# Gate rows and head factors spread by DMA, and the relative-position product moved ahead of the input's transposes

## The chip, the cores and the metric

One core of one Trainium2 chip runs the whole program. The metric is the device time of one execution in microseconds; less is better.

## What is computed

The input x is 256 tokens of 1024 channels in fp32. The first block (block 1) is what the change touches:

```
u = rmsnorm(x) * norm_in;  p = u @ w_in          # 13 projections in one matrix
mLSTM: q, k (4 heads x 128, convolved over 4 tokens, SiLU), v (4 x 256), gates li, lf (4 each)
       num / max(|den|, exp(-m)) per head and token, normalised, times the output gates mo and mz
sparse attention, 8 heads x 64: index score I[t,s] = sum_h w[t,h] relu(iq[t,h] . ik[s]);
       each query attends to its top 64 admissible keys:
       softmax(q.k/8 + rel_bias[bucket(t - s)]) v, times the gate az
out = concat(mLSTM, attention) @ w_out + x, then a gated per-layer input
```

A second block of two layers follows (modulated norms, latent and block-sparse attention, convolved feed-forward), whose modulation vectors silu(c) @ mod_w are worked out in the background during block 1. Nothing of the second block is changed.

## The kernel before

**Tiles.** Activations stand transposed: 8 tiles of 128 channels x 256 tokens (u), each as a high part and the rounding rest. A weight tile is loaded in fp32 (raw, six buffers), cast by ScalarE to its high part (wh, line 174) and subtracted by VectorE to its rest (wl, line 175); four buffers each. A projection tile of 128 output channels is 8 channel blocks times the three products of lines 187 to 189 (high x high, high x rest, rest x high), 24 instructions of 256 columns; where tokens are on the partitions (av, mv) it is lines 213 to 215 with 512 columns. So TensorE needs one split from VectorE and one cast from ScalarE for every 12 products.

**Order.** Up to the ixq projection the order is written out by hand (`manual_schedule`, in block1). From there on a scheduler fixes one list per engine when the kernel is built; each engine goes through its list in order and waits at an instruction until what it reads, and the buffer it writes, is there. Program order and the generator `side()` (line 642), which `tick()` advances after each projection tile, give the scheduler its priorities. The projections run as: ixq (by hand), ikg (index keys and gates), aqk (8 tiles), av, mqk (8 tiles), mv, az (4), mo (8), mz (8).

**Beside the projections.** `side()` makes the gate rows (grow), the gates' running sums and maxima (gr, gB, ga, gM, gbm, lines 656 to 665), sends the maxima through DRAM to all partitions (mscr, mbc, lines 667 and 669, on GpSimd's queue), then the index scores of two query blocks (lines 679 to 688), the transposed gates (gcol), the top-k as eight rounds of MAX and MATCH_REPLACE per block (lines 704, 706) and the mask neg (713, 714). Once av is done it yields one attention stage per tick: logits lg (729), mask plus bias mb on GpSimd (733), the softmax' first step lgs on VectorE (334), exp on ScalarE (335), reciprocal and scaling pr on VectorE (337, 338), then one stage later the transposes ptr (740), pt, and another stage later hav (749, 750). After mv come the mLSTM stages: sums and numerators (mnum, lines 781 to 788), denominators through a transpose (mstT, 806; den, 810 to 814), mrT (820), rrow (822).

**Background.** Each mqk tile is convolved by one ScalarE and three VectorE steps (cv, line 863) and goes through a tanh. A modulation unit either makes 32 products on TensorE (line 983, ps_mod) or, with VectorE, eight accumulations of 1024 columns (modacc, one by ScalarE at line 996, seven by VectorE at line 998) and four products; either way VectorE reads the sum (modr, 1008), TensorE transposes it (modt, 1011) and VectorE copies it (mod, 1013). Its weight tiles (raw_mod) share the six raw buffers with the projections.

**What the change touches.** The gate rows are 8 of the 16 rows of g16 (line 633): two products with rows of the identity bring rows 8 to 11 and 12 to 15 to partitions 0 to 3 in PSUM (646, 647), and VectorE copies them to grow (653). The head factors rrow, 4 x 256, are spread over 128 partitions by four products with a broadcast identity column (826), and VectorE multiplies the eight halves of the numerators by them from PSUM (829). The bias of the relative position is a product of a 32 x 384 one-hot matrix (oh) with the bias table (rb), line 437, copied to relrow (439), sent to DRAM (relscr, 441) and read back as eight shifted 128 x 256 tiles (relb, two DMAs, 445). The names in the lists below carry the scheduler's tile numbers; the numbers of before and after differ by a few for the same tile.

Of the kernel before, what the change touches and what calls it, by code (L numbers as in the profile page):

```python
# [9 lines left out]
F32 = mybir.dt.float32  # L10
# [3 lines left out]
ALU = mybir.AluOpType  # L14
# [4 lines left out]
P = 128  # L19
S = 256  # L20
# [383 lines left out]
def vec(ap, s):  # L404
    return ap.rearrange(s, p=P)
# [3 lines left out]
def setup_first(g):  # L409
    nc, a = g.nc, g.a  # L410
    g.ident = g.mask("ident", 1.0, 0, 1, -1, cmp=ALU.not_equal)
    g.mhalf = g.cp.tile([P, 8], F32, tag="mhalf", name="mhalf")
    nc.gpsimd.memset(g.mhalf, -0.5)
    g.ones = g.cp.tile([P, P], F32, tag="ones", name="ones")
    nc.gpsimd.memset(g.ones, 1.0)


def setup_block1(g):
    nc, a, wk = g.nc, g.a, g.wk
    c = g.columns(g.rows([vec(a["m_norm"][0], "(k p) -> k p"), vec(a["norm_final"], "(k p) -> k p"),  # L420
                   vec(a["conv_w"][0], "j (k p) -> (j k) p")], "0"), "0", "A")
    g.m_norm, g.norm_final = c[:, 0:8], c[:, 8:16]
    g.conv_w = c[:, 16:48].rearrange("p (j k) -> p j k", j=4)
    g.anti = g.mask("anti", 1.0, -(P - 1), 1, 1, cmp=ALU.not_equal, pool=wk)
    g.rmask = g.mask("rmask", -BIG, P - 1, -1, -1, pool=wk)
    g.gbias = wk.tile([16, 1], F32, tag="gbias", name="gbias")
    nc.gpsimd.memset(g.gbias, 0.0)
    nc.sync.dma_start(g.gbias[8:16, :], a["b_gate"][0].rearrange("(k o) -> k o", o=1))
    g.zero4 = g.t1("zero4")[0:4]
    nc.gpsimd.memset(g.zero4, 0.0)  # L430

    oh = g.t3("oh")[0:32]
    rb = wk.tile([32, 8], F32, tag="rb", name="rb")
    nc.sync.dma_start(oh, a["buckets"])
    nc.sync.dma_start(rb, a["rel_bias"])
    ps = g.ps("relb", "A")
    nc.tensor.matmul(ps[0:8, 0:384], rb, oh, start=True, stop=True)
    row = g.t3("relrow")[0:8]
    nc.vector.tensor_copy(row, ps[0:8, 0:384])
    scr = g.dp.tile([8, 384], F32, tag="relscr", name="relscr")  # L440
    nc.gpsimd.dma_start(scr, row)
    g.relb = []
    for e in range(2):
        t = g.b4r(f"relb{e}").rearrange("p (h s) -> p h s", h=4)
        nc.gpsimd.dma_start(t, bass.AP(scr.tensor, scr.offset + 4 * e * 384, [[1, P], [384, 4], [1, S]]))
        g.relb += [t[:, h, :] for h in range(4)]
# [83 lines left out]
def block1(g):  # L530
    nc, a = g.nc, g.a
    V, A, T, G_ = nc.vector, nc.scalar, nc.tensor, nc.gpsimd
# [6 lines left out]
    with g.tc.manual_schedule():  # L539
        for tb in range(2):  # L540
            nc.sync.dma_start(xt[tb], a["x"][0, tb * P:(tb + 1) * P, :])
        norm_in = g.rows([vec(a["norm_in"][0], "(k p) -> k p")], "n", nc.scalar)
        setup_first(g)
        raws = [g.wload(w, 2 * c, 2, 6152, 512, f"ixq{c}") for c in range(4)]
        ws = []
# [33 lines left out]
        for _ in range(WARM):  # L579
            T.matmul(warm[:, 0:P], g.ident, g.ident, start=True, stop=True)  # L580
        g.norm_in = g.columns(norm_in, "n", "M")
        pst = [g.ps(f"xtr{i}", "A") for i in range(4)]

        def trans(k, tb):
# [8 lines left out]
        for k in range(KD):  # L593
# [11 lines left out]
            for e, f in ((0, 0), (0, 1), (1, 0)):  # L605
                for i in range(4):
# [3 lines left out]
                             stop=k == KD - 1 and (e, f) == (1, 0), skip_group_check=True)  # L610
# [8 lines left out]
    nc.sync.dma_start(rv[:, :, 72:80], w[:, 4096:4104].rearrange("(k p) c -> p k c", p=P))  # L619
    hv, lv = g.split(rv, "ikg")  # L620
    setup_block1(g)
    psk = g.ps("ikg", "M")
    for k in range(KD):
# [8 lines left out]
    g16, g16r = g.t1("g16")[0:16], g.t1("g16r")[0:16]  # L632
# [9 lines left out]
    def side():  # L642


        ps = g.ps("grow", "A")
        T.matmul(ps[0:4, 0:S], g.ident[0:16, 8:12], g16, start=True, stop=True)
        T.matmul(ps[0:4, S:2 * S], g.ident[0:16, 12:16], g16, start=True, stop=True)
        for tb in range(2):
            psw = g.ps(f"iwt{tb}", "A")
            T.transpose(psw[:, 0:16], g16r[:, tb * P:(tb + 1) * P], g.ident[0:16, 0:16])  # L650
            V.tensor_scalar(iw[:, tb, :], psw[:, 0:8], 8.0 ** -0.5, 0.125, op0=ALU.mult, op1=ALU.mult)
        grow = g.b2("grow")[0:4]
        V.tensor_copy(grow, ps[0:4, :])
        li, fr = grow[:, 0:S], grow[:, S:2 * S]
        r1, r2, Bc, ar, Mx, bm = (g.t1(n)[0:4] for n in ("gr1", "gr2", "gB", "ga", "gM", "gbm"))
        V.tensor_scalar(r2, fr, -1.0, None, op0=ALU.mult)
# [17 lines left out]
        for tb in range(2):  # L674
            n = (tb + 1) * P
            sc = g.t1(f"sc{tb}")
            for h in range(8):
                ps = g.ps(f"sc{tb}_{h}", "A")
# [12 lines left out]
        ps = g.ps("gcol", "A")  # L691
# [29 lines left out]
        for st in range(10):  # L721
            h = st
            if h < 8:
                lo = 64 * (h % 2)
                ps = g.ps(f"lg{h}", "A")
# [10 lines left out]
            h = st - 1  # L736
# [6 lines left out]
            h = st - 2  # L743
# [16 lines left out]
        for st in range(5):  # L760
            h = st
# [13 lines left out]
            h = st - 1  # L775
# [44 lines left out]
            T.transpose(prt[0:4, tb * P:(tb + 1) * P], rs[:, 4 * tb:4 * tb + 4], g.ident)  # L820
        rrow = g.t1("rrow")[0:4]
        V.tensor_scalar(rrow, prt[0:4, 0:S], 0.25, None, op0=ALU.mult)
        yield
        for h in range(4):
            pb = g.ps(f"mrb{h}", "A")
            T.matmul(pb[:, 0:S], g.ident[0:4, h:h + 1].to_broadcast([4, P]), rrow, start=True, stop=True)
            for vv in range(2):
                t = nums[h][:, vv * S:(vv + 1) * S]
                V.tensor_tensor(t, t, pb[:, 0:S], op=ALU.mult)
            if h % 2:  # L830
                yield

    iw = g.wk.tile([P, 2, 8], F32, tag="iw", name="iw")
    steps = side()
    n_tick = [0]

# [61 lines left out]
    ps = g.ps("ptT", "A")  # L898
# [621 lines left out]
```

## Time and profile before

| | |
|---|---|
| median of 3 runs | 877.22 us (877.14 to 877.37) |
| the profiled execution's own time | 879.18 us |
| its span, first to last instruction | 877.4 us |
| TensorE busy | 859.3 us, 98% |
| VectorE busy | 673.2 us, 77% |
| ScalarE busy | 502.6 us, 57% |
| GpSimd busy | 52.6 us, 6% |
| mean granted TensorE clock | 0.996 of full speed |

The profile covers one execution. Busy time tells how much of the span an engine worked; which engine sets the end of a stretch is read from who waits for whom there. TensorE's products are pipelined, so the price of one is taken from its start to the start of the next, not from its own duration, which reaches over the next one's start. A product of two fp32 operands is recorded twice.

### The profile page before, as it was taken

The page shows a single profiled execution, that of the slowest core. Times are in us where ns is not written, and L with a number is a line of the kernel's source. Part 1 is how long each engine was busy: PE and PEld are TensorE (multiplying, and loading weights), DVE is VectorE, ACT ScalarE, POOL GpSimd, SP SyncE. Part 2 cuts the span into 40 slices and gives each one's busy share as a digit, 9 for nine tenths or more (in the row PEclk, how much of TensorE's full clock was granted, in tenths as well). Part 3 has the DMA queues.
Part 4 walks back from the last instruction along what each step waited for, and adds up shares of the span by engine and source line. Part 5 has one row for each costly group of instructions (what it writes and reads, how often), then busy time and mean ns, then how long its engine had stood idle before and what let it go on. Part 6 is the DMA issues. An engine that isn't in the chain of part 4 may idle for free. (4 is left out here: it accounts for less than half of the span.)

```text
span 877.4 us, 14288 instructions
## 1 busy us (share of the span) xinstructions
PE 859.3 (98%) x5415; PEld 741.1 (84%) x5415; DVE 673.2 (77%) x1289; ACT 502.6 (57%) x925; POOL 52.6 (6%) x81
## 2 busy tenths in 40 slices
PE   9999999999999899999999999999999999999996
PEld 8998779999888688798888888678888988888885
DVE  5798787768767576679899998675866686777786
ACT  6555666445557555377556557276553775565660
POOL 2003111000000131000000000000000000000003
PEclk9999999999999999999999999999999999999999
DMA  8955796854447963498898985498453956566411
GB/s 269 357 197 175 279 345 202 285 211 151 144 150 258 305 250 117 132 377 286 305 331 296 336 290 190 162 345 296 161 176 104 377 178 203 181 220 204 143 49 48
DMA packets 112760, 199.27 MB, mean 227 GB/s; under 512 B 8388, under 2 KB 76468, under 8 KB 112692
## 3 DMA queue, kind: packets, MB, share of 16 engines
q1 hardware_dynamic: 111892, 196.25, 65.7%
q0 software_dynamic: 496, 1.59, 0.5%
q8 instruction: 42, 0.69, 0.3%
q10 hardware_dynamic: 304, 0.53, 0.2%
q14 instruction: 26, 0.21, 0.1%
HBM read 197.28 MB, written 1.08 MB: 226 GB/s over the span
## 5 line engine op out<-in xcount | busy, mean ns | idle before, releaser
L194 PE MATMUL ps_f<-ln,wh_f 128*128 128x512 f32 x576 | 203.8, 396 | 0.0
L195 PE MATMUL ps_f<-ln,wl_f 128*128 128x256 f32 x576 | 161.4, 280 | 0.0
L194 PEld LDWEIGHTS ps_f<-ln,wh_f 128*128 128x128 f32 x576 | 108.1, 188 | 26.5 <-issue 0.8
L195 PEld LDWEIGHTS ps_f<-ln,wl_f 128*128 128x128 f32 x576 | 108.7, 189 | 1.4 <-issue 0.4
L174 ACT CAST wh_fo<-raw_fo 128x1024 fp32r<-128x1024 f32 x38 | 39.9, 1050 | 39.3 <-PE ps_f L194 38.2
L174 ACT CAST wh_f<-raw_fa 128x1024 fp32r<-128x1024 f32 x36 | 37.7, 1051 | 40.8 <-PE ps_f L194 20.3
L175 DVE TENSOR_TENSOR wl_fo<-raw_fo,wh_fo 128x1024 fp32r<-128x1024 f32 x38 | 46.5, 1223 | 19.0 <-ACT wh_fo L174 18.9
L175 DVE TENSOR_TENSOR wl_f<-raw_fa,wh_f 128x1024 fp32r<-128x1024 f32 x36 | 43.9, 1222 | 15.3 <-ACT wh_f L174 15.3
L174 ACT CAST wh_f<-raw_fb 128x1024 fp32r<-128x1024 f32 x36 | 37.1, 1050 | 28.0 <-PE ps_fy L215 17.8
L998 DVE SCALAR_TENSOR_TENSOR modacc<-raw_mod,c,modacc 128x1024 f32<-128x1024 f32 x40 | 51.1, 1278 | 2.0 <-ACT modacc L996 2.0
L175 DVE TENSOR_TENSOR wl_f<-raw_fb,wh_f 128x1024 fp32r<-128x1024 f32 x36 | 43.4, 1221 | 9.2 <-ACT wh_f L174 8.9
L188 PE MATMUL ps_fi<-ln,wh_fi 128*128 128x256 f32 x128 | 35.6, 285 | 0.0
L215 PE MATMUL ps_fy<-wh_fo,fh 128*128 128x512 f32 (+1 forms) x99 | 35.2, 369 | 0.0
L214 PE MATMUL ps_fy<-wl_fo,fh 128*128 128x512 f32 (+1 forms) x99 | 35.1, 368 | 0.0
L189 PE MATMUL ps_fi<-ln,wl_fi 128*128 128x256 f32 x128 | 34.6, 283 | 0.0
L187 PE MATMUL ps_fi<-ln,wh_fi 128*128 128x256 f32 x128 | 34.0, 286 | 0.0
L213 PE MATMUL ps_fy<-wh_fo,fh 128*128 128x512 f32 (+1 forms) x99 | 33.3, 367 | 0.0
L204 DVE TENSOR_TENSOR adf<-ps_f,adf 128x256 f32<-128x256 f32 x72 | 30.0, 417 | 0.0
L983 PE MATMUL ps_mod<-raw_mod,c 128*32 128x256 f32 x400 | 26.9, 383 | 1.0 <-DVE mod L1013 1.0
L203 ACT COPY adf<-ps_f 128x256 f32<-128x256 f32 x72 | 26.1, 363 | 0.0
L174 ACT CAST wh_fi<-raw_fi 128x1024 fp32r<-128x1024 f32 x16 | 17.0, 1079 | 14.9 <-PE ps_mlay L215 8.3
L188 PEld LDWEIGHTS ps_fi<-ln,wh_fi 128*128 128x128 f32 x128 | 24.5, 192 | 0.4 <-DVE ln L377 0.4
(807 smaller groups left out, 2582.4 us busy)
## 6 DMA issues: line engine op xcount, KB each, us to landing
raw_mod<-in_mod_w_dram SPq DMA_DIRECT2D x48, 1024.0 KB
raw_fo<-in_ffn_w_out_dram SPq DMA_DIRECT2D x22, 1024.0 KB
raw_fa<-in_ffn_w_in_dram SPq DMA_DIRECT2D x18, 1024.0 KB
raw_fb<-in_ffn_w_in_dram SPq DMA_DIRECT2D x18, 1024.0 KB
raw_fi<-in_ffn_w_in_dram SPq DMA_DIRECT2D x16, 512.0 KB
raw_wo<-in_w_out_dram SPq DMA_DIRECT2D x6, 1024.0 KB
raw_aqk<-in_w_in_dram SPq DMA_DIRECT2D x4, 1024.0 KB
raw_mqk<-in_w_in_dram SPq DMA_DIRECT2D x4, 1024.0 KB
```

Source lines behind the costliest of these rows:

```text
L174: self.nc.scalar.copy(hv, src)
L175: self.nc.vector.tensor_tensor(lv, src, hv.bitcast(F32), op=ALU.subtract)
L187: T.matmul(ps, wh, xh, start=start, stop=False, skip_group_check=chk)
L188: T.matmul(ps, wh, xl, start=False, stop=False, skip_group_check=chk)
L189: T.matmul(ps, wl, xh, start=False, stop=stop, skip_group_check=chk)
L194: T.matmul(ps, wh, x[2], start=start, stop=False, skip_group_check=True)
L195: T.matmul(ps[:, 0:S], wl, x[0], start=False, stop=stop, skip_group_check=True)
L204: V.tensor_tensor(t, ps[:, 0:S], t, op=ALU.add)
L213: T.matmul(ps, xh, wh, start=start, stop=False)
L214: T.matmul(ps, xh, wl, start=False, stop=False)
L215: return T.matmul(ps, xl, wh, start=False, stop=stop)
L998: nc.vector.scalar_tensor_tensor(st["acc"], rv[:, e], c, st["acc"], op0=ALU.mult, op1=ALU.add)
```

## The change

The two loads of the relative position move from SyncE's queue to ScalarE's, and are issued early; the product, its copy and its three DMAs move from setup_block1 into the part whose order is written by hand, behind the column transposes of norm_in and ahead of the transposes of x. The two products for the gate rows and the copy give way to two DMAs from g16 to grow on GpSimd's queue. The four products for the head factors give way to a DMA of rrow to DRAM (rscr) and one that reads it back to all partitions (mrbc, 128 x 1024), both on GpSimd's queue; the eight multiplications read mrbc in SBUF. Lines below the edits have numbers higher by 8 to 10 in the changed kernel.

```diff
--- before.py
+++ after.py
@@ -429,11 +429,19 @@
     g.zero4 = g.t1("zero4")[0:4]
     nc.gpsimd.memset(g.zero4, 0.0)
 
-    oh = g.t3("oh")[0:32]
-    rb = wk.tile([32, 8], F32, tag="rb", name="rb")
-    nc.sync.dma_start(oh, a["buckets"])
-    nc.sync.dma_start(rb, a["rel_bias"])
-    ps = g.ps("relb", "A")
+
+def relative_load(g):
+
+    oh, rb = g.t3("oh")[0:32], g.wk.tile([32, 8], F32, tag="rb", name="rb")
+    g.nc.scalar.dma_start(oh, g.a["buckets"])
+    g.nc.scalar.dma_start(rb, g.a["rel_bias"])
+    return oh, rb
+
+
+def relative(g, oh, rb):
+
+    nc = g.nc
+    ps = g.ps("relb", "V")
     nc.tensor.matmul(ps[0:8, 0:384], rb, oh, start=True, stop=True)
     row = g.t3("relrow")[0:8]
     nc.vector.tensor_copy(row, ps[0:8, 0:384])
@@ -540,6 +548,7 @@
         for tb in range(2):
             nc.sync.dma_start(xt[tb], a["x"][0, tb * P:(tb + 1) * P, :])
         norm_in = g.rows([vec(a["norm_in"][0], "(k p) -> k p")], "n", nc.scalar)
+        buckets = relative_load(g)
         setup_first(g)
         raws = [g.wload(w, 2 * c, 2, 6152, 512, f"ixq{c}") for c in range(4)]
         ws = []
@@ -579,6 +588,7 @@
         for _ in range(WARM):
             T.matmul(warm[:, 0:P], g.ident, g.ident, start=True, stop=True)
         g.norm_in = g.columns(norm_in, "n", "M")
+        relative(g, *buckets)
         pst = [g.ps(f"xtr{i}", "A") for i in range(4)]
 
         def trans(k, tb):
@@ -642,15 +652,13 @@
     def side():
 
 
-        ps = g.ps("grow", "A")
-        T.matmul(ps[0:4, 0:S], g.ident[0:16, 8:12], g16, start=True, stop=True)
-        T.matmul(ps[0:4, S:2 * S], g.ident[0:16, 12:16], g16, start=True, stop=True)
+        grow = g.b2("grow")[0:4]
+        for e in range(2):
+            nc.gpsimd.dma_start(grow[:, e * S:(e + 1) * S], g16[8 + 4 * e:12 + 4 * e, :])
         for tb in range(2):
             psw = g.ps(f"iwt{tb}", "A")
             T.transpose(psw[:, 0:16], g16r[:, tb * P:(tb + 1) * P], g.ident[0:16, 0:16])
             V.tensor_scalar(iw[:, tb, :], psw[:, 0:8], 8.0 ** -0.5, 0.125, op0=ALU.mult, op1=ALU.mult)
-        grow = g.b2("grow")[0:4]
-        V.tensor_copy(grow, ps[0:4, :])
         li, fr = grow[:, 0:S], grow[:, S:2 * S]
         r1, r2, Bc, ar, Mx, bm = (g.t1(n)[0:4] for n in ("gr1", "gr2", "gB", "ga", "gM", "gbm"))
         V.tensor_scalar(r2, fr, -1.0, None, op0=ALU.mult)
@@ -820,13 +828,15 @@
             T.transpose(prt[0:4, tb * P:(tb + 1) * P], rs[:, 4 * tb:4 * tb + 4], g.ident)
         rrow = g.t1("rrow")[0:4]
         V.tensor_scalar(rrow, prt[0:4, 0:S], 0.25, None, op0=ALU.mult)
+        rscr = g.dp.tile([4, S], F32, tag="rscr", name="rscr")
+        nc.gpsimd.dma_start(rscr, rrow)
+        rb_ = g.b4r("mrbc").rearrange("p (h s) -> p h s", h=4)
+        nc.gpsimd.dma_start(rb_, bass.AP(rscr.tensor, rscr.offset, [[0, P], [S, 4], [1, S]]))
         yield
         for h in range(4):
-            pb = g.ps(f"mrb{h}", "A")
-            T.matmul(pb[:, 0:S], g.ident[0:4, h:h + 1].to_broadcast([4, P]), rrow, start=True, stop=True)
             for vv in range(2):
                 t = nums[h][:, vv * S:(vv + 1) * S]
-                V.tensor_tensor(t, t, pb[:, 0:S], op=ALU.mult)
+                V.tensor_tensor(t, t, rb_[:, h, :], op=ALU.mult)
             if h % 2:
                 yield
```

**The order on each engine.** The scheduler makes its lists anew, and in block 1 they differ in more than the edited lines. Three places are shown as the lists have them: line, operation, output<-input, shape.

TensorE, behind the third or fourth mqk tile. ps_mod are the first modulation unit's products, ps_modt the transposes of its sum, ptr and lg those of the attention, ps_mqk the projection. Before:

```order
L188 MATMUL ps_mqk_1135<-u_77,wh_mqk_0_1136 128x256
L189 MATMUL ps_mqk_1135<-u_77,wl_mqk_0_1137 128x256
L983 MATMUL ps_mod_1207<-raw_mod_1205,c 32x256 x5
L740 MATMUL ps_ptr_1056<-anti,pr_977 128x128
L729 MATMUL ps_lg_1103<-ak,aq 128x128
L729 MATMUL ps_lg_1103<-ak,aq 128x256
L983 MATMUL ps_mod_1207<-raw_mod_1205,c 32x256 x3
L187 MATMUL ps_mqk_1218<-u_74,wh_mqk_0_1219 128x256
L188 MATMUL ps_mqk_1218<-u_74,wh_mqk_0_1219 128x256
```

With the change:

```order
L188 MATMUL ps_mqk_1062<-u_77,wh_mqk_0_1063 128x256
L189 MATMUL ps_mqk_1062<-u_77,wl_mqk_0_1064 128x256
L993 MATMUL ps_mod_1205<-raw_mod_1203,c 32x256 x8
L993 MATMUL ps_mod_1205<-raw_mod_1357,c 32x256 x8
L993 MATMUL ps_mod_1205<-raw_mod_1510,c 32x256 x8
L993 MATMUL ps_mod_1205<-raw_mod_1571,c 32x256 x8
L1021 MATMUL ps_modt_1585<-ident,modr_1581 128x128 x2
L187 MATMUL ps_mqk_1133<-u_74,wh_mqk_0_1134 128x256
L188 MATMUL ps_mqk_1133<-u_74,wh_mqk_0_1134 128x256
```

The 32 products stood in pieces of 5, 3, 5, 3, 12 and 4 from the fourth mqk tile on to the first mv tile, with attention stages among them; now they stand in one block behind the third mqk tile, directly followed by the transposes, which need VectorE's modr.

VectorE, the end of the top-k. wl are the splits of the weights, cv the convolution. Before:

```order
L704 MAX m_1_7_870<-tk_6_864 128x8
L706 MATCH_REPLACE tk_7_872<-m_1_7_870,tk_6_864 128x256
L713 TENSOR_SCALAR neg_890<-tk_7_868 128x128
L713 TENSOR_SCALAR neg_893<-tk_7_872 128x256
L714 TENSOR_TENSOR neg_890<-neg_890,rmask 128x128
L714 TENSOR_TENSOR neg_893<-neg_893,rmask 128x128
L175 TENSOR_TENSOR wl_mqk_0_1137<-raw_mqk_1062,wh_mqk_0_1136 128x1024
L175 TENSOR_TENSOR wl_mqk_0_1220<-raw_mqk_1216,wh_mqk_0_1219 128x1024
L863 SCALAR_TENSOR_TENSOR cv_966<-cx_965,cols_317,cv_966 128x255
L863 SCALAR_TENSOR_TENSOR cv_966<-cx_965,cols_317,cv_966 128x254
L863 SCALAR_TENSOR_TENSOR cv_966<-cx_965,cols_317,cv_966 128x253
L175 TENSOR_TENSOR wl_mqk_0_1291<-raw_mqk_1216,wh_mqk_0_1290 128x1024
```

With the change, first the place of modr in the top-k, then its end:

```order
L714 MATCH_REPLACE tk_5_834<-m_1_5_832,tk_4_826 128x256
L714 MATCH_REPLACE tk_6_858<-m_0_6_856,tk_5_830 128x128
L1018 SCALAR_TENSOR_TENSOR modr_1581<-ps_mod_1205,modb_1582 128x256
L712 MAX m_1_6_860<-tk_5_834 128x8
L712 MAX m_0_7_864<-tk_6_858 128x8
```

```order
L714 MATCH_REPLACE tk_7_870<-m_1_7_868,tk_6_862 128x256
L721 TENSOR_SCALAR neg_888<-tk_7_866 128x128
L721 TENSOR_SCALAR neg_891<-tk_7_870 128x256
L722 TENSOR_TENSOR neg_888<-neg_888,rmask 128x128
L722 TENSOR_TENSOR neg_891<-neg_891,rmask 128x128
L873 SCALAR_TENSOR_TENSOR cv_964<-cx_963,cols_331,cv_964 128x255
L873 SCALAR_TENSOR_TENSOR cv_964<-cx_963,cols_331,cv_964 128x254
L873 SCALAR_TENSOR_TENSOR cv_964<-cx_963,cols_331,cv_964 128x253
L1008 SCALAR_TENSOR_TENSOR modacc_1626<-raw_mod_1624,c,modacc_1626 128x1024
L334 ISA lgs_974,sm_0_980<-ps_lg_973,mb_0_978 128x128
L334 ISA sm_0_980 128x1
```

Before, the splits of the mqk tiles stood among and right behind the last rounds, and modr came 79 rows later. Now seven of the eight mqk tiles' splits stand ahead of modr, modr stands in the seventh of the eight rounds, and the convolution, a modulation accumulation and the first softmax follow its end directly.

VectorE, where the numerators are multiplied. Before:

```order
L822 TENSOR_SCALAR rrow<-ps_mrT 4x256
L1008 SCALAR_TENSOR_TENSOR modr_2245<-ps_mod_2240,modb_2246 128x256
L175 TENSOR_TENSOR wl_mz_0_2372<-raw_mz_2332,wh_mz_0_2371 128x1024
L829 TENSOR_TENSOR mnum_1825<-mnum_1825,ps_mrb_2228 128x256 x2
L829 TENSOR_TENSOR mnum_1907<-mnum_1907,ps_mrb_2232 128x256 x2
L1013 COPY mod_2252<-ps_modt_2249 128x2x4
L829 TENSOR_TENSOR mnum_1969<-mnum_1969,ps_mrb_2289 128x256 x2
L829 TENSOR_TENSOR mnum_2017<-mnum_2017,ps_mrb_2293 128x256 x2
L175 TENSOR_TENSOR wl_mz_0_2410<-raw_mz_2406,wh_mz_0_2409 128x1024
L175 TENSOR_TENSOR wl_mz_0_2446<-raw_mz_2406,wh_mz_0_2445 128x1024
L175 TENSOR_TENSOR wl_mz_0_2484<-raw_mz_2480,wh_mz_0_2483 128x1024
L889 SCALAR_TENSOR_TENSOR mzt_2363<-mzt_2363,ps_mz_2334 128x256
```

With the change:

```order
L830 TENSOR_SCALAR rrow<-ps_mrT 4x256
L1018 SCALAR_TENSOR_TENSOR modr_2243<-ps_mod_2238,modb_2244 128x256
L175 TENSOR_TENSOR wl_mz_0_2366<-raw_mz_2326,wh_mz_0_2365 128x1024
L1023 COPY mod_2250<-ps_modt_2247 128x2x4
L175 TENSOR_TENSOR wl_mz_0_2404<-raw_mz_2400,wh_mz_0_2403 128x1024
L839 TENSOR_TENSOR mnum_1823<-mnum_1823,mrbc 128x256 x2
L839 TENSOR_TENSOR mnum_1905<-mnum_1905,mrbc 128x256 x2
L839 TENSOR_TENSOR mnum_1967<-mnum_1967,mrbc 128x256 x2
L839 TENSOR_TENSOR mnum_2015<-mnum_2015,mrbc 128x256 x2
L175 TENSOR_TENSOR wl_mz_0_2440<-raw_mz_2400,wh_mz_0_2439 128x1024
L175 TENSOR_TENSOR wl_mz_0_2478<-raw_mz_2474,wh_mz_0_2477 128x1024
L899 SCALAR_TENSOR_TENSOR mzt_2357<-mzt_2357,ps_mz_2328 128x256
```

The eight multiplications stood behind the second mz split and ahead of the third; now the third split comes ahead of them, and two splits stand between them and the first gated tile instead of three.

## Rows read from the trace of the kernel before

**Rows 1.** The page's list of engines: busy time, share of the span and instructions of each.

```profile
PE 859.3 (98%) x5415; PEld 741.1 (84%) x5415; DVE 673.2 (77%) x1289; ACT 502.6 (57%) x925; POOL 52.6 (6%) x81
```

**Rows 2.** What TensorE waited for over the whole span (view of waits): the waiting product, what it waited on, us in total, times, longest. The largest entry, and two of block 1.

```profile
PE ps_mlv L213 <- ACT krx L1221: 2.6, 1, 2.6
PE ps_aqk L187 <- DVE ixq L612: 0.4, 1, 0.4
PE ps_xtr L586 <- ACT xs L572: 0.2, 1, 0.2
```

**Rows 3.** Busy time in stretches: us, then PE, PEld, DVE, ACT and POOL busy us (instructions), granted clock, DMA share, GB/s.

```profile
10.00:60.00 50.00, 49.62 (x378) 46.43 (x377) 40.98 (x90) 29.21 (x54) 4.33 (x8) 1.00 0.86 280
60.00:80.00 20.00, 20.00 (x128) 17.70 (x127) 18.81 (x52) 11.13 (x17) 7.05 (x8) 1.00 0.57 179
```

**Rows 4.** TensorE in order of time, the identity products of the gate rows (start us, us, line, output<-input) and the first instruction behind them.

```profile
30.99 0.59 PE L646 MATMUL ps_grow<-g,ident 16*4 16x256 f32 x2
31.94 0.29 PE L650 MATMUL ps_iwt<-ident,g16r 16*128 16x16 f32 x2
```

**Rows 5.** TensorE in order of time, the two pairs of products that spread rrow, and the projection product behind the first pair.

```profile
178.05 1.12 PE L826 MATMUL ps_mrb<-rrow,ident 4*128 4x256 f32 x4
179.11 0.39 PE L187 MATMUL ps_mo<-u,wh_mo 128*128 128x256 f32 x1
180.59 1.12 PE L826 MATMUL ps_mrb<-rrow,ident 4*128 4x256 f32 x4
```

**Rows 6.** TensorE in order of time, the relative-position product and the projection behind it.

```profile
16.77 0.81 PE L437 MATMUL ps_relb<-oh,rb 32*8 32x384 f32 x2
17.50 0.62 PE L609 MATMUL ps_ixq<-u,wh_ixq 128*128 128x256 f32 x3
```

**Rows 7.** TensorE in order of time: the three column transposes, the first logits of the attention, a stretch of 48 projection products, and the first five modulation products (an fp32 product is two records), and the first probability transpose behind them.

```profile
53.90 0.38 PE L398 MATMUL ps_cols<-ident,rows 76*128 76x76 f32 x3
70.89 0.92 PE L729 MATMUL ps_lg<-ak,aq 64*128 64x128 f32 x4
71.74 0.38 PE L187 MATMUL ps_mqk<-u,wh_mqk 128*128 128x256 f32 x1
75.66 0.38 PE L187 MATMUL ps_mqk<-u,wh_mqk 128*128 128x256 f32 x1
81.60 1.05 PE L983 MATMUL ps_mod<-raw_mod,c 128*32 128x256 f32 x10
82.58 0.33 PE L740 MATMUL ps_ptr<-anti,pr 128*128 128x128 f32 x1
```

**Rows 8.** VectorE in order of time between the columns and the fourth but last mqk split: the column copies, the convolution's three steps, and what ended its idle time (in brackets).

```profile
54.31 0.54 DVE L400 COPY cols<-ps_cols 128x76 f32<-128x76 f32 x3
71.96 1.49 DVE L175 TENSOR_TENSOR wl_mqk<-raw_mqk,wh_mqk 128x1024 fp32r<-128x1024 f32 x1 [1.03 <-ACT wh_mqk L174]
73.38 2.44 DVE L863 SCALAR_TENSOR_TENSOR cv<-cx,cols,cv 128x255 f32<-128x255 f32 x3
79.87 1.21 DVE L175 TENSOR_TENSOR wl_mqk<-raw_mqk,wh_mqk 128x1024 fp32r<-128x1024 f32 x1
```

**Rows 9.** VectorE in order of time, from which prices are taken, start to start: one round of the top-k for both query blocks (60.01 to 61.18), a split (wl, it starts at 118.14 as well) up to a modulation accumulation (modacc), which runs up to the softmax' first step on 256 columns (lgs), scaled probabilities (pr) and a convolution step (cv).

```profile
60.01 0.61 DVE L704 MAX8 m<-tk 128x8 f32<-128x256 f32 x2
61.18 1.22 DVE L175 TENSOR_TENSOR wl_mqk<-raw_mqk,wh_mqk 128x1024 fp32r<-128x1024 f32 x1
118.14 0.08 DVE L334 DVE_READ_ACCUMULATOR2_ANT sm<- 128x1 f32 x1
119.28 1.28 DVE L998 SCALAR_TENSOR_TENSOR modacc<-raw_mod,c,modacc 128x1024 f32<-128x1024 f32 x1
120.47 0.42 DVE L334 CUSTOM_DVE_ANT_0 lgs<-ps_lg,mb 128x256 f32<-128x256 f32 x1
120.81 0.08 DVE L334 DVE_READ_ACCUMULATOR2_ANT sm<- 128x1 f32 x1
124.96 0.26 DVE L338 TENSOR_SCALAR pr<-pr,smr 128x128 f32<-128x128 f32 x1
125.14 0.47 DVE L863 SCALAR_TENSOR_TENSOR cv<-cx,cols,cv 128x255 f32<-128x255 f32 x1
125.54 0.34 DVE L338 TENSOR_SCALAR pr<-pr,smr 128x256 f32<-128x256 f32 x1
```

**Rows 10.** GpSimd in order of time, the DMAs that it issues (relscr, relb, mbc; relb and mbc wait for the landing of what they read), and the landing of mbc from its issue.

```profile
18.46 0.75 POOL L441 DMA_DIRECT2D relscr<-relrow  x1 [10.48 <-DVE relrow L439]
22.81 1.56 POOL L445 DMA_DIRECT2D relb<-relscr  x2 [2.58 <-DMA relscr<-relrow]
45.73 0.57 POOL L669 DMA_DIRECT2D mbc<-mscr  x1 [5.30 <-DMA mscr<-gM]
DMA to landing us min/median/max: 6.2/6.2/6.2
```

**Rows 11.** A modulation load: its issue on SyncE, and the ScalarE instruction that uses it.

```profile
84.83 1.31 SPq L159 DMA_DIRECT2D raw_mod<-in_mod_w_dram  x1
92.42 1.15 ACT L996 ACTIVATE modacc<-raw_mod,c 128x1024 f32<-128x1024 f32 x1 [1.01 <-DMA raw_mod<-in_mod_w_dram]
```

**Rows 12.** VectorE and TensorE where the mLSTM's numerators are scaled: the first four multiplications, and the first product of the gate projection.

```profile
178.78 1.42 DVE L829 TENSOR_TENSOR mnum<-mnum,ps_mrb 128x256 f32<-128x256 f32 x4 [0.99 <-PE ps_mrb L826]
184.62 0.28 PE L187 MATMUL ps_mz<-u,wh_mz 128*128 128x256 f32 x1
```

## The prediction

> **What bounds the kernel now.** The page's list of engines comes first: TensorE is busy 98% of the span, VectorE 77% [rows 1]. The reader should then ask whether anybody makes TensorE wait, and where. The view of waits answers: the largest entry of the span is 2.6 us, and in block 1, where every edit lies, the projections waited 0.4 us for VectorE and the transposes 0.2 us for ScalarE [rows 2]. By stretches TensorE is busy 49.62 of 50 us and then 20.00 of 20 [rows 3]. So in block 1 a product that is taken away is time won, and work on another engine costs nothing as long as that engine keeps up. VectorE is the one to watch: from 60 to 80 us it was busy 18.81 of 20 us [rows 3]. The clock was 1.00 in these stretches, so one price per product holds.
>
> **What is removed.** On TensorE three things go away, each priced from its start to the start of the instruction behind it. The gate rows: 30.99 to 31.94, 0.95 us [rows 4]. The four products that spread rrow: 178.05 to 179.11, 1.06 us for a pair, and the second pair at 180.59 has the same 1.12 us of busy time, so 2.12 us [rows 5]. The relative-position product sat between two projections, 16.77 to 17.50, 0.73 us [rows 6]; it is not removed but put in front of the transposes, where TensorE waited 0.2 us [rows 2] and where the first projection needs u, which ScalarE and VectorE make from the transposed tiles. There it could cost from 0 to its own 0.73; I take 0, as the transposes run ahead of the copies that follow them. Sum: -3.80 us. The VectorE copy of the gate rows goes too and is worth nothing by itself.
>
> **What is added on queues.** The two loads on ScalarE's queue stand ahead of its first work and cost nothing unless they land late (a rival below). The grow DMAs are two on GpSimd's queue, with nothing waiting behind them there until mscr. Their nearest row is a landing of 6.2 us [rows 10]; the gates that read them now stand behind the first split of av on VectorE, later than that, so 0. The two for rrow are on a path. The nearest rows give the chain: from the issue of relscr to that of relb 4.35 us; mbc waited 5.30 for mscr, whose issue I count like mbc's own, 0.57; then 6.2 from the issue of mbc to its landing [rows 10]. I count from the transposes mrT: rrow ends 0.8 later, the first issue comes at 1.1, the second at 5.5 to 7.0, landing at 11.7 to 13.2. VectorE does in that time the splits of mz 0 to 2 and then stands still: the eight multiplications (1.42 for four [rows 12], 2.84) end at 14.5 to 16.0, two splits and the first gated tile, 2.3 + 0.4, at 17.2 to 18.7. TensorE reaches the fourth mz tile, whose bank the first gated tile frees, after 14 + 5 x 24 projection products at about 0.12 (below), with a few small ones 16.5 us. So TensorE waits 0.7 to 2.2 us where the products needed no wait; I take 1.3.
>
> The Trainium skill ("DMA: Bandwidth & Descriptors", section "Anatomy of one DMA — SWDGE (gpsimd) path") gives about 2.0 us plus bytes at 436 GB/s for such a DMA. By that page an estimate for both is some 5 us, mrbc would be there early, and this term would be 0 rather than 1.3; the trace shows 6.2 for one [rows 10], so I go by the trace.
>
> **What is moved.** This is the largest part, and the diff doesn't show it: the scheduler orders block 1 anew. Two places decide. On TensorE the 32 products of the first modulation unit stand in one block behind the third mqk tile, where they were spread up to the first mv tile; the index scores, gcol and the columns have gone from the aqk tiles to the av and mqk tiles. On VectorE the top-k follows them. Before, TensorE had 28.7 us between the columns (53.90) and the first probability transpose (82.58) [rows 7], filled with 24 aqk, 48 av and 96 mqk products; after the change 92 mqk and the 32 modulation products stand there. VectorE needed nearly all of the 28.7 us: the columns' copies start at 54.31, and up to 79.87 it stood still little more than the 1.03 us of one wait [rows 8].
>
> The sum goes from the last of the 32 products. VectorE's modr reads them, and behind it stands, up to the scaled probabilities that the third stage's transposes on TensorE need (rows 111 to 181 of its new order): 1.5 rounds of top-k at 1.17, 1.75; four splits at 1.14, 4.56; seven accumulations modacc at 1.19, 8.33; 14 convolution steps at 0.40, with four multiplications like them, 7.1; four stages' first steps at 0.34 and about 0.2, 2.2; scaled probabilities 4 x 0.18 and 3 x 0.26 (an estimate between 0.18 and 0.34), 1.5; reciprocals, neg and modr, about 2.0 [rows 9]. That is 27.4 us. The same prices set on the rows from 54.3 to 79.87 give 21.8, where the trace took 25.5 with some 1.2 of standing still: the trace is 10% above them (three convolution steps took 2.44 there, not 1.2 [rows 8]), so up to 30.2.
>
> TensorE has in the same time 120 projection products at 0.124 (48 of them took 75.66 to 81.60), 14.9; three logits at 0.85; two hav of about 0.75 (an estimate by the logits); nine transposes at 0.13; four modulation products at 0.2 (five took 0.98) and the modt, together 21.2 us [rows 7]. So TensorE must wait 6.2 us by the bare prices and 9.0 by the raised ones; I take 7.6, between them. Nothing behind it gives it back: TensorE had no idle time in block 1 to lend [rows 3].
>
> A load comes on top. The raw_mod tile of the last two accumulations can be issued only when the second split of mv has freed its buffer, 4.9 to 5.4 us of VectorE work ahead of its use. A load issued at 84.83 was used at 92.42, after a wait of 1.01 for it, so 7.6 us [rows 11]: 0 to 2.7 us of waiting. I take 0.7, since that row's load stood right behind another one.
>
> **Sum.** -3.80 + 1.3 + 7.6 + 0.7 = +5.8 us. The profiled execution took 879.18 us (span 877.4), 1.96 over the median; set on the median of 877.22 the forecast is 883.0 us. Its own range: 877.22 - 3.8 + 6.2 + 0.7 = 880.3 to 877.22 - 3.8 + 9.0 + 2.7 + 2.2 = 887.3.
>
> **Rivals.**
> - *Cover holds (the other side).* VectorE stays ahead of the transposes, since ScalarE or VectorE in this order takes less than 21.2 us for what I price at 27.4, or because fewer rows really stand ahead of the probabilities. For it: VectorE is idle for 23% of the span [rows 1], so the total fits. Against it: both orders are fixed lists, and TensorE can't pass a transpose that waits. It decides if VectorE's work is 23% under its price. Then -3.8 with 0 to 1.3 for mrbc: 873.4 to 874.7.
> - *Half of the wait.* The wait is 2 to 5.5 us because TensorE itself comes late to the 32 products (it needs their last load) while VectorE goes on with the top-k: 877.22 - 3.8 + 2 to 5.5 = 875.4 to 878.9, mostly no difference.
> - *Loads late.* The wait on raw_mod tiles comes at two accumulations, or at the 32 products too, each up to 2.7: 887 to 890.
> - *oh late.* The product ahead of the transposes holds all of them until the loads from ScalarE's queue land. Block 1 then starts later by that time, us for us; one landing of 6.2 [rows 10] after an issue near 2 us is the time of the transposes, so 0 to 2 us: 883 to 885 with the forecast's other terms.
> - *Starved descriptors.* The mrbc DMAs take longer than the 6.2 us of the row, as they come while VectorE is at work: 2 to 5 us more on the mrbc term, 885 to 888. A page of the Trainium skill speaks for it ("SBUF — State Buffer", section "SBUF: two separate sides"): a DMA from GpSimd's queue can be held up while VectorE has the port that both share. The trace doesn't bear it out so far: mbc was issued with VectorE busy and landed in 6.2 [rows 10].
>
> That the products are not taken away is no case: they are gone from TensorE's list.
>
> **How the numbers follow.** Forecast 0.66, loads late 0.07, oh late 0.04, starved 0.05: slower. Cover holds 0.10: faster. Half of the wait 0.08: mostly within 0.2%, which is 1.75 us and about what a measurement of this kernel can tell from no change. So slower 0.82, same 0.07, faster 0.11. The range reaches from 878.5, into the upper end of the half wait, to 888.5, into late loads and starved descriptors; it leaves out cover holds and the tails.
>
> **What would show it.** In the changed profile: no ps_grow and no ps_mrb on TensorE; TensorE waiting some 6 to 12 us in all on scaled probabilities, modacc or the convolution's cx between the 32 modulation products and the first mv tile, with VectorE at 95% there; a wait of 0.7 to 2.2 us at the fourth mz tile, with VectorE waiting on the mrbc DMA. It is wrong if TensorE is at 20 of 20 us in that stretch, or if a wait of several us stands ahead of the transposes.

## The result and the profile after

The changed kernel takes 886.39 us (median of 4 runs, 885.71 to 887.02) against 877.22: 1.0101 times the time of before, 95% interval 1.0086 to 1.0116. It is slower, as forecast, at 886.4 instead of 883.0. The profiled execution took 887.02 us (span 885.2), 7.84 over that of before; the medians differ by 9.17, as the profiled execution was 1.96 over its median before and 0.63 over it with the change. The ledger below explains the profiles.

The list of engines, beside [rows 1]: TensorE works 2.8 us less, and the span is 7.8 longer.

```profile
PE 856.5 (97%) x5403; PEld 741.1 (84%) x5403; DVE 672.2 (76%) x1288; ACT 503.0 (57%) x925; POOL 55.9 (6%) x85
```

The view of waits, the entries of TensorE that differ from before by over 0.5 us (us in total, times, longest). Before, block 1 had nothing over 0.4 [rows 2]; now cx, pr, modr (1.0 of its 1.5), mzt and wl_wo stand there. The wait at mlv, in the second block, was 2.6 and is 2.1.

```profile
PE ps_mqk L187 <- ACT cx L869: 5.3, 4, 3.9
PE ps_ptr L748 <- DVE pr L338: 2.7, 3, 1.6
PE ps_mlv L213 <- ACT krx L1231: 2.1, 1, 2.1
PE ps_modt L1021 <- DVE modr L1018: 1.5, 2, 1.0
PE ps_mz L187 <- DVE mzt L899: 1.1, 1, 1.1
PE ps_wo L214 <- DVE wl_wo L175: 0.7, 1, 0.7
```

The same columns as [rows 3], by stretch. TensorE is still full from 60 to 80 us, with less work on VectorE and the DMAs than before; then it loses 6.44 and 2.91 us while VectorE and the DMAs are busier than in the first stretch.

```profile
60.00:80.00 20.00, 20.00 (x160) 16.97 (x162) 16.69 (x50) 11.67 (x20) 0.00 (x0) 1.00 0.48 157
80.00:100.00 20.00, 13.56 (x105) 11.59 (x97) 17.94 (x55) 8.69 (x19) 7.37 (x10) 0.91 0.88 321
100.00:120.00 20.00, 17.09 (x107) 13.65 (x108) 19.43 (x47) 11.81 (x31) 3.86 (x4) 1.00 0.76 244
```

**The longest wait.** TensorE needs the PSUM bank that ScalarE's cx copy frees. In order of time, VectorE's convolution steps of the tile before and then ScalarE: the accumulation, first of the second modulation unit, waits 8.26 us for its load, and th and cx stand behind it. The convolution is done at 87.01 and th starts at 88.84, so 1.83 us of TensorE's wait are due to the load and the accumulation, and the 2.04 ahead of them to VectorE.

```profile
85.08 1.93 DVE L873 SCALAR_TENSOR_TENSOR cv<-cx,cols,cv 128x255 f32<-128x255 f32 x3
87.79 1.15 ACT L1006 ACTIVATE modacc<-raw_mod,c 128x1024 f32<-128x1024 f32 x1 [8.26 <-DMA raw_mod<-in_mod_w_dram]
88.84 0.40 ACT L875 ACTIVATE th<-cv 128x256 f32<-128x256 f32 x1
89.15 0.35 ACT L869 COPY cx<-ps_mqk 128x256 f32<-128x256 f32 x1
```

SyncE's issues show why the load is late. The 32 products in one block (77.63 to 81.42) hold the raw buffers until TensorE gets there, and then four loads start within 2.8 us, from 78.76 on. The load of 75.18 is the fourth of the first unit; so the one waited for is that of 79.63.

```profile
75.18 0.37 SPq L159 DMA_DIRECT2D raw_mod<-in_mod_w_dram  x1
78.76 0.37 SPq L159 DMA_DIRECT2D raw_mv<-in_w_in_dram  x1
79.63 0.37 SPq L159 DMA_DIRECT2D raw_mod<-in_mod_w_dram  x1
80.49 0.37 SPq L159 DMA_DIRECT2D raw_mv<-in_w_in_dram  x1
81.48 0.37 SPq L159 DMA_DIRECT2D raw_mod<-in_mod_w_dram  x1
```

TensorE in order of time, where that wait ends, and then the stretches of 2 us around it. After the 3.87 us of waiting the granted clock is 0.50, which is 1.2 GHz: the 14 products from 89.55 to the next one's start at 92.71 take 3.16 us, where the first 14 behind a later wait, at full clock, take 1.78 (95.67 to 97.45), so **1.38 us more**.

```profile
89.55 0.58 PE L187 MATMUL ps_mqk<-u,wh_mqk 128*128 128x256 f32 x1 [3.87 <-ACT cx L869]
```

```profile
86.00:88.00 2.00, 0.00 (x0) 0.00 (x0) 0.98 (x2) 0.21 (x1) 2.00 (x4) 1.00 1.05 396
88.00:90.00 2.00, 0.45 (x2) 0.45 (x3) 1.03 (x1) 1.97 (x4) 1.11 (x3) 0.83 1.04 406
90.00:92.00 2.00, 2.00 (x11) 2.00 (x11) 2.00 (x9) 1.54 (x5) 1.12 (x2) 0.50 0.82 250
92.00:94.00 2.00, 2.00 (x16) 1.95 (x14) 2.00 (x4) 0.44 (x3) 0.21 (x1) 0.82 1.00 359
```

**What sets the end of the stretch.** From the last of the 32 products (81.42) to the end of the scaled probabilities that the last of the nine waits is for (114.06), VectorE is busy 30.32 of 32.64 us, and from 89.55 on 24.26 of 24.51. It is idle almost only for the load: 1.96 us behind ScalarE's accumulation and 0.25 for a later tile. TensorE has 23.43 us of work there, 22.05 without the clock's 1.38. So VectorE sets the end, and at the full clock TensorE would have waited those 1.38 us instead (this is argued from the rows; no run has the same order at the full clock). The two stretches, then VectorE's waits in the first:

```profile
81.42:114.06 32.64, 23.43 (x159) 20.11 (x159) 30.32 (x78) 15.84 (x39) 10.50 (x13) 0.95 0.83 288
89.55:114.06 24.51, 20.13 (x133) 17.02 (x133) 24.26 (x57) 14.11 (x36) 6.59 (x7) 0.94 0.76 249
```

```profile
DVE modacc L1008 <- ACT modacc L1006: 2.0, 1, 2.0
DVE modacc L1008 <- DMA raw_mod<-in_mod_w_dram: 0.3, 1, 0.3
```

**The head factors.** GpSimd's issues, VectorE's multiplication (before: [rows 12]) and TensorE's wait. From the issue of mrbc to the first use it is 8.2 us, where [rows 10] had 6.2.

```profile
184.01 0.59 POOL L832 DMA_DIRECT2D rscr<-rrow  x1 [4.53 <-DVE rrow L830]
187.12 0.57 POOL L834 DMA_DIRECT2D mrbc<-rscr  x1 [2.52 <-DMA rscr<-rrow]
195.31 1.09 DVE L839 TENSOR_TENSOR mnum<-mnum,mrbc 128x256 f32<-128x256 f32 x3 [5.21 <-DMA mrbc<-rscr]
200.74 0.39 PE L187 MATMUL ps_mz<-u,wh_mz 128*128 128x256 f32 x1 [1.14 <-DVE mzt L899]
```

**The moved product.** TensorE; beside [rows 6]. The transposes now start at 8.78, 0.71 us later than before (8.07); ixq starts 0.58 later (10.66, 10.08), and the first aqk product 0.23 earlier (26.41, 26.64).

```profile
8.05 0.81 PE L445 MATMUL ps_relb<-oh,rb 32*8 32x384 f32 x2
8.78 1.64 PE L596 MATMUL ps_xtr<-ident,xs 128*128 128x128 f32 x13
```

**Ledger**, us, from first starts on TensorE and its waits: grow -0.95 [rows 4], factors -2.12 [rows 5], relb -0.23; waits from 80 to 116 us +9.35 (nine); clock +1.38; mz +1.14; wo +0.66; the old wait at mlv 0.55 shorter. Sum +8.68; TensorE's last product starts 7.81 later (877.05, 869.24). The 0.87 between lies ahead of the first mo product: from the first aqk product to it TensorE is busy 127.18 us, 125.80 without the clock's 1.38, where the 127.64 of before less grow's 0.95 make 126.69. So the same work is done in less time in the new order; which products save it was not traced.

### The profile page after: what moved, and what is told of

Read it like the earlier page. It is cut to its first block, busy times and chain, and to the rows that moved or that the text cites. A ratio compares the mean times of both kernels' runs of the same rounds, so it can differ in the third digit from the quotient of the medians.

```text
span 885.2 us, 14277 instructions
## 1 busy us (share of the span) xinstructions
PE 856.5 (97%) x5403; PEld 741.1 (84%) x5403; DVE 672.2 (76%) x1288; ACT 503.0 (57%) x925; POOL 55.9 (6%) x85
```

## Experiments

Each is timed against the kernel before; ratios are with their 95% interval. The theory: the gate rows' DMA makes the scheduler put the gate work and scores late, and this new order costs all of the loss. The rivals: the factors' DMA, the moved product, or the late loads alone.

**1. Gate rows alone by DMA**, on the kernel before (its other parts untouched). The edit is the grow part of the change.

> The kernel before with only the gate rows by DMA; the relative-position product and the head factors as before. Theory 1 (the grow DMA makes the scheduler put the index scores, the top-k and the 32 modulation products later, and that order costs some 8.5 us, which is the changed kernel's delay at the first mz product, 6.2, with 0.2 and 2.1 of the other two parts taken back): 885 to 886.5 us, with TensorE waits of 9 to 10 us between 80 and 120 us, the largest for ScalarE's cx. Rival (the three parts share the loss, or the added DMAs cost by themselves): 877 to 881 us. Rival (grow is a gain of its product time alone): 876.3 us.

886.31 us, 1.0096 (1.0083 to 1.0110): the whole loss, with TensorE's wait at cx again 3.8 us long. Two deleted products, 0.95 us together, cost 8.8 us by the order that follows.

**2. The changed kernel without that part** (gate rows by the two products again).

> The changed kernel with the gate rows by products again; relative-position product in front and head factors by DMA stay. Theory 1: the order of block 1 is nearly that of before, so no stall in the mqk stretch: 877.2 - 0.2 - 2.1 + 1.1 to 2.0 for the wait on the first gated tile and behind it = 876 to 877. Rival (the moved product and the head factors' DMA carry a good part of the loss): 879 to 883.

877.64 us, 1.0000 (0.9991 to 1.0009), 0.6 above the range expected, and the loss is gone. No wait is left between 80 and 116; at mz 1.48 us are waited and at wo 0.56.

**3. All the DMAs, other order.** In side() the index scores are written ahead of the gates (the code is abridged).

```diff
+    <index scores of both query blocks>
     li, fr = grow[:, 0:S], grow[:, S:2 * S]
     ...
     nc.gpsimd.dma_start(mb_, ...)
     yield
-    <index scores of both query blocks>
```

> The changed kernel, all DMAs as in it, but in the program the index scores are written ahead of the gates' sums, and the gates behind them. The lists then have the attention and the modulation products where the kernel before has them, from the first mqk tile on. Theory 1 (the order costs, not the DMA): 877.2 - 0.95 - 0.2 - 2.1 + 1.1 to 2.0 = 875 to 876. Rival (the DMA of grow itself, its landing, or the loads' contention costs): 880 to 886, as the changed kernel.

877.28 us, 0.9995 (0.9987 to 1.0004), no stall in the mqk stretch: it is the order, not the transfer, that costs. (In the changed kernel, too, grow lands 6.2 to 6.5 us after its issue near 29, and is first read at 44.5.) 875 to 876 was expected: of the 3.3 us that the products and the move took away little is left in the median (the profiled execution, at 876.09, is the fastest of twelve); mz waits 1.24 us.

**4. The factors alone by DMA**, on the kernel before.

> The kernel before with only the head factors by DMA. By the forecast's terms: 877.2 - 2.12 + 1.1 (the wait at the fourth mz tile that the changed kernel's trace has, 1.14) = 876.2. If the 0.66 us wait at wo and the small ones behind mz in the changed kernel come from this part too: 877 to 877.5. If the DMA's chain is longer without the other edits: 878 or more.

878.31 us, 1.0006 (0.9997 to 1.0014). The first mz product comes 1.82 us earlier, then TensorE waits 2.00 at mz and the clock falls again (stretches of 2 us; the wait ends at 193.59, in the first):

```profile
192.00:194.00 2.00, 0.41 (x3) 0.41 (x4) 1.96 (x4) 0.00 (x0) 0.00 (x0) 1.00 0.76 277
194.00:196.00 2.00, 2.00 (x13) 2.00 (x13) 1.97 (x4) 1.51 (x3) 0.00 (x0) 0.62 0.83 311
196.00:198.00 2.00, 2.00 (x12) 2.00 (x11) 1.97 (x4) 0.53 (x2) 0.00 (x0) 0.52 0.95 311
```

**5, 6. Experiment 3 with the factors by products, and by DMAs issued on ScalarE's queue.**

```diff
-nc.gpsimd.dma_start(rscr, rrow)
+nc.scalar.dma_start(rscr, rrow)
...
-nc.gpsimd.dma_start(rb_, ...)
+nc.scalar.dma_start(rb_, ...)
```

> Scores first, gate rows by DMA, relative-position product in front, but the head factors by the four products again. If the wait for mrbc (TensorE stood 1.2 us at the fourth mz tile) and the halved clock that a longer wait there brings (seen with the factors alone: 2.0 us of waiting and 1.7 us at a clock of 0.5 to 0.6) eat up what the products gave, this is as fast or faster than with the DMA: 877.5 - 0.95 - 0.3 = 876.2, and its runs spread less. If the head factors' DMA is a gain of 2.1 less 1.2: 878.2.

> Scores first as before, with rscr and mrbc issued on ScalarE's queue instead of GpSimd's; the lists of the engines are otherwise the same. If the queue makes the landing long (8.2 us for mrbc from its issue): VectorE's wait of 5.3 us shrinks, TensorE's 1.2 us goes, 875 to 876. If the landing is the transfer's own (128 rows of 4 KB read from DRAM while loads of 1 MB run): landing stays 7 to 9 us, time stays 877.3.

By products 876.40 us, 0.9991 (0.9982 to 1.0000), as expected; on ScalarE's queue **874.27 us**, 0.9964 (0.9952 to 0.9977), faster than both kernels and than the 875 to 876 expected. The issues there, SyncE's 1 MB load of raw_wo, and VectorE's multiplications:

```profile
174.89 0.26 ACTq L829 DMA_DIRECT2D rscr<-rrow  x1
176.81 0.36 ACTq L831 DMA_DIRECT2D mrbc<-rscr  x1
178.16 0.43 SPq L159 DMA_DIRECT2D raw_wo<-in_w_out_dram  x1
181.18 2.77 DVE L836 TENSOR_TENSOR mnum<-mnum,mrbc 128x256 f32<-128x256 f32 x8
```

The multiplications follow a split without a wait, so mrbc was there at most 4.4 us after its issue. In experiment 3, by GpSimd's queue, it came 8.2 after:

```profile
177.88 0.43 SPq L159 DMA_DIRECT2D raw_wo<-in_w_out_dram  x1
177.96 0.57 POOL L831 DMA_DIRECT2D mrbc<-rscr  x1 [2.51 <-DMA rscr<-rrow]
186.22 1.10 DVE L836 TENSOR_TENSOR mnum<-mnum,mrbc 128x256 f32<-128x256 f32 x3 [5.31 <-DMA mrbc<-rscr]
```

The first hop, from the issue of rscr to that of mrbc, is 1.9 us on ScalarE's queue and 3.1 on GpSimd's, and so mrbc stands 1.35 us ahead of raw_wo in the one and 0.08 behind it in the other. GpSimd's queue by itself does not make the 8.2 us: in experiment 12 below, the same transfer on that queue, with a 1 MB load issued 2.4 us ahead of it and SyncE's next one at 188.40, lands in 4.1 (the first hop, beside that load, takes 4.9).

```profile
178.76 0.37 SPq L159 DMA_DIRECT2D raw_mz<-in_w_in_dram  x1
181.17 0.57 POOL L834 DMA_DIRECT2D mrbc<-rscr  x1 [4.32 <-DMA rscr<-rrow]
185.26 2.77 DVE L839 TENSOR_TENSOR mnum<-mnum,mrbc 128x256 f32<-128x256 f32 x8 [3.65 <-DMA mrbc<-rscr]
```

So what is issued just ahead makes most of the 8.2 us. No run moved that load alone.

**7. The factors alone by DMA, on ScalarE's queue**, on the kernel before: the edit of 6 on 4.

> The kernel before with the head factors alone spread by DMA, both transfers issued on ScalarE's queue. Theory (the factors' products are worth the 2.1 us that the mz landmark gave, and GpSimd's queue lost it again as a wait for the late broadcast): the broadcast lands within 4 us, VectorE's wait for it is under 1 us, no wait of TensorE at the mz products, total 875.3 (874.6 to 876). Rival (the factors' spread by DMA gives nothing whatever the queue): 877 to 878.5, with a wait at mz or a later one in its place.

875.38 us, 0.9976 (0.9967 to 0.9986), no wait at mz: 1.85 us less than the kernel before, of the products' 2.12, and the interval holds all of it. So the removed products pay once the broadcast is early.

**8. Experiment 6 with the relative-position product at its old place.**

> Scores first, gate rows by DMA, head factors by DMA on ScalarE's queue, but the relative-position product at its old place and its loads on SyncE's queue. If moving the product in front gains its 0.73 us: 875.0. If it gains the 0.2 us that the first aqk product showed (26.64 before, 26.41 changed): 874.5. If it gains nothing: 874.3.

874.83 us, 0.9969 (0.9958 to 0.9981): by the ratios moving it is worth some 0.4 us, which is not clear of noise, as the intervals of 6 and 8 overlap.

**9 to 12. What makes the stall**, all on the changed kernel. First ScalarE's accumulation on VectorE, then VectorE's accumulations at a quarter of the columns (three quarters of those sums are left out), then the second unit's loads of half the size (the second half of each is left out, the first used twice), and last the second unit moved out of the stretch.

```diff
-nc.scalar.mul(st["acc"], rv[:, e], c)
+nc.vector.tensor_scalar(st["acc"], rv[:, e], c, None, op0=ALU.mult)
```

> The changed kernel with the first step of a modulation accumulation on VectorE instead of ScalarE, so that ScalarE doesn't wait for the raw_mod load ahead of the copy cx that frees a projection's bank. Theory A (the 3.87 us wait of TensorE and the halved clock behind it come from ScalarE standing behind the load): that wait falls to 2.1 us or less (VectorE's cv is ready 1.8 us ahead of the load) and the total by 2 to 3.5 us, 883 to 884.5. Theory B (VectorE's list sets the end of the stretch whatever ScalarE does): the waits move from cx to the probabilities, the first mv product comes at the same time as in the changed kernel (116.3) or later, and the total stays at 886 to 887.5.

888.89 us, 1.0133 (1.0119 to 1.0147). Inconclusive: the scheduler put VectorE's accumulation, which waits 1.60 us for the load, ahead of the convolution's third step; the wait at cx grew to 4.8.

```diff
-nc.vector.scalar_tensor_tensor(st["acc"], rv[:, e], c, st["acc"], ...)
+nc.vector.scalar_tensor_tensor(st["acc"][:, 0:S], rv[:, e, 0:S], c, st["acc"][:, 0:S], ...)
```

> The changed kernel with VectorE's modulation accumulations cut from 1024 to 256 columns (so three quarters of these sums are left out); loads, products and ScalarE's part stay. In the mqk stretch VectorE's work falls by 7 x 0.9 = 6.3 us. Theory B (VectorE's sum limits): the waits of 9.35 us between 80 and 116 us fall by about 6, first mv product near 110.5. Theory A (the load and ScalarE): the wait at cx of 3.9 us and the halved clock stay, the waits behind it (4.5 us in all) go, first mv product near 112.

884.48 us, 1.0080 (1.0064 to 1.0095). A wait of 3.86 at cx stays, and the clock is at 0.50 until 94.4, longer than in the changed kernel; the waits after it shrink from 4.5 us in all to 0.25, and the first mv product comes at 111.46 instead of 116.34. So those later waits are VectorE's accumulations, and the first is not. The total falls by 1.9 us only: in the profiled execution 2.4 us are lost again in the second block, between 408 and 578 us, and the cause was not traced.

```diff
-... k, 2, D * m, D, ...)
+... k, 1 if (i, m) == (0, 0) else 2, D * m, D, ...)
```

> The changed kernel with the four loads of the second modulation unit halved to 0.5 MB (each half is used twice, so half of that unit's weights are left out); VectorE's and ScalarE's accumulations stay as they are. In the changed kernel four loads of 1 MB are issued between 78.8 and 81.5 us at some 400 GB/s in all, and ScalarE waits 8.26 us for the second of them. Theory A (that bunch is what holds ScalarE, and behind it cx and TensorE): 3 MB instead of 4 land some 2 us earlier, the wait at cx falls from 3.9 to 1.5 to 2.5 us and the clock may not fall; the waits behind it grow a little, as VectorE's work is the same; 884 to 885.5. If the load doesn't matter for the sum (VectorE's list limits): 886 to 887, with the waits moved.

892.33 us, 1.0169 (1.0155 to 1.0182): a miss. The lists changed with it (ScalarE's accumulation now ahead of cv, VectorE's ahead of convolution steps), and the wait at cx is 5.3; it tells nothing on the load's share.

```diff
-if n_tick[0] >= 16 and n_tick[0] % 2 == 0 and (0, 2) not in g.have:
+if (16 <= n_tick[0] < 24 or n_tick[0] >= 34) and n_tick[0] % 2 == 0 and ...:
```

> The changed kernel with the second modulation unit's loads and accumulations skipped at the ticks that fall into the index-score stretch and done at later ticks instead; the sums are the same, the order of the gate and score products is like the changed kernel's. Theory (the gate rows' DMA puts the order's gate block ahead of the scores; ScalarE's accumulation then waits 8.3 us for its load ahead of cx, and VectorE carries 8.3 us of accumulations in the same 20 us): without the unit no load wait stands on ScalarE, TensorE's waits between 80 and 116 us fall from 9.35 to 0 to 2 us, the clock stays at 0.99 or above there, the first mv product starts at 105 to 107; the total is 876 to 880, according to what the unit costs where it now runs. Rival (the late scores and selection alone cost the time, whatever the unit does): waits of over 4 us stay between 80 and 116, total 882 or more.

882.53 us, 1.0055 (1.0041 to 1.0069): between the two, the total as the rival has it and the waits nearer to the theory. TensorE's waits from 80 to 116 us fall to 3.44 (modr 1.03, cx 2.15, pr 0.26), mv starts at 108.63 instead of 116.34, and where the unit now runs, around the output projection, 3.2 us are waited (1.02, 0.96, 1.22). ScalarE and then TensorE in order of time, with the stretch behind:

```profile
86.77 0.42 ACT L875 ACTIVATE th<-cv 128x256 f32<-128x256 f32 x1 [7.58 <-DVE cv L873]
87.09 0.35 ACT L869 COPY cx<-ps_mqk 128x256 f32<-128x256 f32 x1
87.49 0.47 PE L187 MATMUL ps_mqk<-u,wh_mqk 128*128 128x256 f32 x1 [2.15 <-ACT cx L869]
```

```profile
88.00:90.00 2.00, 2.00 (x11) 2.00 (x11) 2.00 (x8) 1.80 (x5) 2.00 (x4) 0.50 1.09 356
```

With no load in the way, th still waits for VectorE's cv, which stands behind the late top-k. Of the 3.87 us about 2.15 are thus the late top-k and 1.7 the load (an estimate, from two kernels; the changed kernel's own rows above give 2.04 and 1.83).

## Why the prediction was right, and where its sizes were off

- **The place and the cause: shown.** TensorE stands still behind the 32 products, and experiments 1 to 3 put the loss on the order that the gate rows' DMA brings, not on the transfer and not on the other two parts. "Cover holds" and "half of the wait" fall. Why the scheduler chooses this order was not looked at.
- **The order, 7.6 us forecast, 8.3 measured.** The sum set VectorE's work against TensorE's between the same two points. VectorE's was forecast at 27.4 us, 30.2 raised, and is 30.32; TensorE's at 21.2, and is 22.05 at the full clock. So the raised price was the right one. The waits fell on other instructions than in the sum, which let TensorE wait for scaled probabilities only (its list of signs names cx): longest for cx (5.3), behind VectorE's top-k and convolution, and for the probabilities only 2.7.
- **The load, 0.7 us forecast, 2.3 measured** as VectorE's idle time. The prediction looked for it at the last two accumulations. It came at the unit's first one, and on ScalarE, whose queue behind that instruction holds th and cx. "Loads late" was right in kind, and the step that was mis-sized is this term: the prediction named what waits for the load but not what is queued behind it on ScalarE.
- **The clock, 0 forecast.** Behind the longest wait products cost 1.38 us more, though not as a loss of their own, since VectorE sets the end. The prediction used one price per product because the clock was 1.00 in the stretches of [rows 3]. The trace of before shows it falling elsewhere, behind the 2.6 us wait of [rows 2], in the stretches of 2 us from 300:

```profile
299.30 0.50 PE L213 MATMUL ps_mlv<-wh_ukv,ckh 128*128 128x512 f32 x1 [2.63 <-ACT krx L1221]
```

```profile
300.00:302.00 2.00, 2.00 (x7) 1.33 (x6) 2.00 (x4) 1.13 (x3) 1.33 (x3) 0.58 1.00 372
302.00:304.00 2.00, 2.00 (x7) 1.58 (x6) 1.29 (x3) 0.00 (x0) 1.31 (x1) 0.56 1.24 292
```

- **mrbc, 1.3 us forecast, 1.14 measured**, but by luck, out of two errors that cancel: the first hop took 3.1 us, not 4.4 to 5.9, and the broadcast 8.2, not 6.2. "Starved descriptors" has its long landing, yet not by the cause that the Trainium skill gives ("SBUF — State Buffer", section "SBUF: two separate sides"): VectorE was busy for only 1.40 of those 8.2 us (0.17 and 1.23). By the Trainium skill ("DMA: Bandwidth & Descriptors", section "Anatomy of one DMA — SWDGE (gpsimd) path") an estimate for the 512 KB is 3.2 us; the trace disagrees, by 2.5 times.
- **relb, -0.73 us forecast, -0.23 measured** (experiment 8 can't tell it from nothing). Ahead of the transposes it was not free: they started 0.71 later. "oh late" is not what happened; the product's own time is.
- **Not in the sum:** the wait at wo (+0.66), a shorter one at mlv (-0.55), and the 0.87 that TensorE's own work is shorter in the new order. With all terms as measured, the two profiles differ by 7.8 us where the sum had 5.8; the medians differ by 1.3 more.

## What to carry to other kernels

When a scheduler orders the engines, a deleted or added instruction is priced by the two orders, not by its own time: read the lists for what is queued behind every instruction that can wait, and on all engines. Where a stall is foreseen, price the products right behind it at the half clock as well, and ask whether another engine's list sets the end anyway. A broadcast through DRAM costs its two landings, and they depend on what is issued just ahead of it; issue it ahead of a large load, not right behind one.

## What the runs showed of the hardware

Ten waits of TensorE of 2.00 to 5.28 us in full work (among them 2.63 at mlv before and 2.08 with the change) each had a granted clock near 0.50 (1.2 GHz) during them or right behind them. Of twelve waits between 1.4 and 1.8 us one had it, 1.78 us at mlv in experiment 9; two others of 1.78, in experiment 11, had not.

The same 512 KB broadcast on GpSimd's queue landed in 8.2 to 8.9 us with a 1 MB load issued 0.06 to 0.4 us ahead of it and smaller ones around (seven kernels), and in 4.1 with such a load 2.4 us ahead and none beside it (experiment 12). mbc, of the same size and on the same queue, landed in 4.5 to 4.7 us where it was issued 0.6 to 0.8 ahead of such a load (four kernels), and in 5.8 to 6.3 where it was issued 0.5 to 2.1 behind one. On ScalarE's queue, 1.3 us ahead of the load, the broadcast was there within 4.5.
